# Narrow experts' postponed split and a final layer norm without GpSimd in a backbone layer with 32 experts

## The chip, the cores and the metric

The kernel runs on one core of a Trainium2 chip. The metric is the device time of one execution in microseconds. Engines are named TensorE (PE; its weight loads are PEld), VectorE (DVE), ScalarE (ACT), GpSimd (POOL) and SyncE (SP, which here only starts DMAs).

## The reference

One layer on 1024 latent tokens of width 1024: a state space branch and a window attention branch, a residual and a layer norm, then a mixture of 32 experts (4 per token), a second residual and the last layer norm. What the change touches is this end:

```python
gu = xb @ w_gate_up[e] + b_gate_up[e]
glu, lin = jnp.split(gu, 2, axis=-1)
act = glu * jax.nn.sigmoid(SWIGLU_ALPHA * glu) * (lin + 1)   # after limits
return act @ w_down[e] + b_down[e]
...
h_new = layer_norm(DEEPNORM_ALPHA * h_new + g2 * ffn, ln2_g[l], ln2_b[l])
```

## The kernel before

The experts are sorted by how many tokens they have. Experts with room for more than 128 rows (ranks 0 to 14) are **wide**, the others have room for 128 and are **narrow**. `ORDER` takes them as 0, 31, 1, 30, ...: wide and narrow in turn, and at the end three narrow ones in a row. Each expert has 12 steps, `c` = 0 to 11, one for each chunk of 1 MB of its weights: eight gate/up chunks, then four down chunks.

Everything is computed in fp32 by parts. A chunk comes in two halves of 512 KB (`raw<-w_gate_up`, `raw<-w_down`, L1515, SyncE, into eight buffers). `Weights.prepare` splits each half: ScalarE copies it to the hi part `wh` (L1532), VectorE subtracts to get the lo part `wl` (L1534); that frees the raw buffer, and the next load may start. There are four buffers of split chunks: three chunks are prepared ahead, so step `c` prepares chunk `c + 3`, counted on into the next expert. TensorE multiplies hi by hi, lo by hi and hi by lo (L1347, L1348, L1350; wide up chunks L1400, L1401).

The orders of TensorE, VectorE and ScalarE are the program's (`manual_schedule`); SyncE's and GpSimd's are put by a scheduler. In each step `weave` takes one piece of each job in turn: the expert's own work `cur.after(c)`, `W.prepare()`, the next expert's x parts (`put`, L1325 and L1327, at c = 1, 6, 7, 10) and, in early experts, list building. Then `cur.main(c)` issues the matmuls:

```python
cur.before(c)
weave(prev.store(1) if c == 0 and prev else None, cur.after(c), W.prepare(), x, limit(to_lists, 1))
...
cur.main(c, W.ready.pop(0))
```

In a narrow expert each half of the activation is finished at c = 4 and c = 8 (`act`, L1385 and L1386 on VectorE, which read the result of the up chunks before). At c = 5 and c = 9 `before` has TensorE transpose it (`tp<-ident,t`, L1318), and `after` splits the transposed half (ScalarE L1325, VectorE L1327, `a<-tp,a`). Down chunks 8 and 9 use the first half, 10 and 11 the second.

An expert's rows are added to the result in HBM by GpSimd's indirect DMA (`acc_d<-y,tab`, L1483) at c = 0 of the next expert. The index tables of later experts (`tab<-list_d`, L1672) are loaded on SyncE's queue into five buffers, each free when the scatter that used it is over.

`finish` is the last layer norm, in four groups of two tiles of 128 rows: SyncE loads the tiles, VectorE makes the statistics (L78, L79) and the inverse root by small operations (`rsqrt`, L61 to L72), ScalarE normalizes (L1842), VectorE multiplies by the gain (L1843), GpSimd adds the bias (L1844), SyncE stores (L1845).

## Time and profile before

| | |
|---|---|
| median of 3 runs | 2726.91 us (2722.59 to 2729.72) |
| the profiled execution | 2724.81 us, span 2723.0 us |
| TensorE busy in the span | 2470.5 us (91%) |
| VectorE busy | 2136.4 us (78%) |
| ScalarE busy | 1480.4 us (54%) |
| GpSimd busy | 312.5 us (11%) |
| expert loop, first wide up matmul to last down matmul | 1100.64 to about 2655 us |
| final layer norm, first load to the end | 2670.97 to 2723.0 us |

Times in rows are microseconds from the start of the span. Busy shares are a mean over stages of different kinds; what a wait costs is read in its stage. A row of waits names the engine and line that waited, the one that ended the wait, and then total us, times, longest us. A row of a timeline gives start, duration, engine, line, operation, out<-in, count, and in brackets the idle time before it with what ended it. In a timeline "SPq" rows are DMAs being put on the queue.

### The profile page before, as it was taken

Reading aid. Unit: us, or ns where it says so; the run is one execution under the profiler, and the core shown is the slowest. Engines: PE = TensorE matmul, PEld = TensorE weight load, DVE = VectorE, ACT = ScalarE, POOL = GpSimd, SP = SyncE. Lnnn points to the kernel's source line nnn. Section 1 sums busy time; section 2 is a strip of 40 time slices with the busy share of each in tenths; the row PEclk is TensorE's granted clock in tenths of the full one; section 3 lists DMA queues with packets and bytes.
Section 4 is the critical chain, followed back from the end, with each engine's and each line's share of the span. In section 5 each row is a group of like instructions: output and inputs, shape, how many; then the busy total and the mean of one; then the engine's idle time right before and its main releaser. Section 6 shows DMA issues by size and latency. Waiting matters only on the chain. (4 is left out here: it accounts for less than half of the span.)

```text
span 2723.0 us, 40435 instructions
## 1 busy us (share of the span) xinstructions
PE 2470.5 (91%) x13750; PEld 2105.6 (77%) x13750; DVE 2136.4 (78%) x3818; ACT 1480.4 (54%) x2375; POOL 312.5 (11%) x205
## 2 busy tenths in 40 slices
PE   6799899888989987799999999999999999999990
PEld 2598887777778876678888888879878887888880
DVE  9635798237778868787988887988888898888995
ACT  0622112657757512555656666766666676667661
POOL 3300000000000004012220100111011011101003
PEclk8799999988999877899999999999999999999995
DMA  7534623544587672787978988988988999999984
GB/s 247 175 119 150 211 88 112 176 151 157 211 303 263 234 272 88 241 263 233 289 242 271 311 250 280 322 270 268 318 282 260 322 304 290 282 335 309 313 291 147
DMA packets 409699, 657.00 MB, mean 241 GB/s; under 512 B 42144, under 2 KB 213024, under 8 KB 403904
## 3 DMA queue, kind: packets, MB, share of 16 engines
q1 hardware_dynamic: 396160, 610.25, 67.3%
q0 software_dynamic: 12896, 42.54, 6.8%
q8 instruction: 110, 1.80, 0.3%
q10 hardware_dynamic: 432, 1.57, 0.2%
q14 instruction: 101, 0.83, 0.1%
HBM read 565.05 MB, written 89.88 MB: 241 GB/s over the span
## 5 line engine op out<-in xcount | busy, mean ns | idle before, releaser
L1534 DVE TENSOR_TENSOR wl<-raw,wh 128x1024 fp32r<-128x1024 f32 x768 | 923.6, 1219 | 202.3 <-ACT wh L1532 189.4
L1532 ACT ACTIVATE wh<-raw 128x1024 fp32r<-128x1024 f32 x768 | 795.3, 1053 | 296.9 <-PE dn L1350 77.8
L1400 PE MATMUL uw<-x,wh 128*128 128x320 f32 (+5 forms) x1920 | 576.7, 364 | 0.2 <-issue 0.2
L1401 PE MATMUL uw<-x,wl 128*128 128x192 f32 (+4 forms) x1920 | 500.3, 261 | 0.0
L1400 PEld LDWEIGHTS uw<-x,wh 128*128 128x128 f32 x1920 | 362.9, 189 | 24.0 <-issue 0.3
L1401 PEld LDWEIGHTS uw<-x,wl 128*128 128x128 f32 x1920 | 368.1, 192 | 0.6
L1347 PE MATMUL dn<-wh,a 128*128 128x512 f32 (+4 forms) x752 | 297.9, 396 | 0.0
L1348 PE MATMUL dn<-wl,a 128*128 128x512 f32 (+4 forms) x752 | 294.6, 392 | 0.0
L1350 PE MATMUL dn<-wh,a 128*128 128x512 f32 (+3 forms) x608 | 239.7, 394 | 0.6 <-DVE a L1327 0.6
L1347 PE MATMUL up<-wh,x 128*128 128x512 f32 x544 | 217.8, 400 | 0.0
L1350 PE MATMUL up<-wh,x 128*128 128x512 f32 x544 | 213.0, 391 | 0.0
L1348 PE MATMUL up<-wl,x 128*128 128x512 f32 x544 | 212.0, 390 | 0.0
L1412 ACT ACTIVATE t<-uw,bias 128x160 f32<-128x160 f32 (+5 forms) x240 | 97.9, 420 | 136.8 <-PE uw L1401 136.6
L1347 PEld LDWEIGHTS dn<-wh,a 128*128 128x128 f32 (+4 forms) x752 | 136.6, 182 | 34.6
L1348 PEld LDWEIGHTS dn<-wl,a 128*128 128x128 f32 (+4 forms) x752 | 136.5, 182 | 34.5
L1483 POOL DMA_INDIRECT acc_d<-y,tab x35 | 80.5, 2299 | 566.9 <-DVE y L1481 463.6
L1350 PEld LDWEIGHTS dn<-wh,a 128*128 128x128 f32 (+3 forms) x608 | 113.5, 187 | 28.8 <-DVE a L1327 3.1
L1350 PEld LDWEIGHTS up<-wh,x 128*128 128x128 f32 x544 | 102.1, 188 | 22.1
L1347 PEld LDWEIGHTS up<-wh,x 128*128 128x128 f32 x544 | 102.5, 188 | 20.2
L1348 PEld LDWEIGHTS up<-wl,x 128*128 128x128 f32 x544 | 102.3, 188 | 19.6
L51 PE MATMUL mm<-whi,uh 128*128 128x256 f32 x320 | 108.3, 338 | 4.5 <-DVE r L308 4.5
L52 PE MATMUL mm<-wlo,uh 128*128 128x256 f32 x320 | 107.5, 336 | 0.0
(544 smaller groups left out, 4934.2 us busy)
## 6 DMA issues: line engine op xcount, KB each, us to landing
raw<-w_gate_up SPq DMA_DIRECT2D x512, 512.0 KB
raw<-w_down SPq DMA_DIRECT2D x256, 512.0 KB
mw<-w_mod SPq DMA_DIRECT2D x64, 256.0 KB
raw<-w_in SPq DMA_DIRECT2D x13, 1024.0 KB
raw<-w_mod SPq DMA_DIRECT2D x8, 1024.0 KB
gate_d<-gs SPq DMA_DIRECT2D x16, 512.0 KB
raw<-w_o SPq DMA_DIRECT2D x8, 1024.0 KB
x<-xhat_d SPq DMA_DIRECT2D x28, 256.0 KB
```

Of the source, the lines that this page charges most:

```text
L51: nc.tensor.matmul(out, lhsT=lsel(lh, k), rhs=rsel(rh, k), start=start and k == 0, stop=False)
L52: nc.tensor.matmul(out, lhsT=lsel(lh, k), rhs=rsel(rl, k), start=False, stop=False)
L1347: nc.tensor.matmul(ps, lhsT=h, rhs=wh[:, k], start=st, stop=False)
L1348: nc.tensor.matmul(ps, lhsT=h, rhs=wl[:, k], start=False, stop=en and nb <= 64)
L1350: nc.tensor.matmul(ps, lhsT=X[:, k0 + k, lo:lo + nb], rhs=wh[:, k], start=False, stop=en)
L1400: nc.tensor.matmul(p[:, 0:2 * n], lhsT=wh[:, k, fs], rhs=self.x[:, k, 0:2 * n], start=k == 0, stop=False)
L1401: nc.tensor.matmul(p[:, 0:m], lhsT=wl[:, k, fs], rhs=self.x[:, k, 0:m], start=False, stop=k == KT - 1)
L1412: nc.scalar.activation(out=y[i], in_=self.uw[i][:, 1], func=ACTF.Identity, bias=self.bias[:, q * 8 + j0 + i:q * 8 + j0 + i + 1])
L1483: nc.gpsimd.indirect_dma_start(out=K.acc_d, out_offset=bass.IndirectOffsetOnAxis(ap=wi[0:nb], axis=0), in_=o[0:nb], in_offset=None, bounds ...
L1532: nc.scalar.activation(out=h, in_=r, func=ACTF.Copy)
L1534: nc.vector.tensor_tensor(l, r, h, ALU.subtract)
```

## The change

In the expert loop, a narrow expert no longer prepares a chunk at c = 7; the next wide expert prepares two at c = 2, and `owed` keeps the count (the narrow expert at place 29 of the order is the last that postpones). At c = 8 and c = 9 of a narrow expert its own work is issued to the end before the weights are split. In `finish` all tiles are loaded first, three of them from ScalarE's queue; VectorE makes the statistics of the even tiles, ScalarE those of the odd ones by sums; the four even and the four odd inverse roots are each made at once; and VectorE does the rest in two scalar_tensor_tensor per tile, the last tile in two halves.

```diff
--- before.py
+++ after.py
@@ -1705,6 +1705,7 @@
                 weave(W.prepare())
                 cur.constants()
             prev = None
+            owed = False
             to_lists = spread(tc, K, P.li)
             with tc.manual_schedule(engines={mybir.EngineType.PE, mybir.EngineType.DVE, mybir.EngineType.Activation}):
                 for i in range(len(ORDER)):
@@ -1714,7 +1715,16 @@
                             ls = next(lists(i + 2, oh) or iter(()), None)
                         x = next(xs, None) if c in (1, 6, 7, 10) else None
                         cur.before(c)
-                        weave(prev.store(1) if c == 0 and prev else None, cur.after(c), W.prepare(), x, limit(to_lists, 1))
+                        late = not cur.wide and c == 7 and not owed
+                        owed = owed or late
+                        if not cur.wide and c in (8, 9):
+                            weave(cur.after(c))
+                            weave(W.prepare(), x, limit(to_lists, 1))
+                        else:
+                            weave(prev.store(1) if c == 0 and prev else None, cur.after(c), None if late else W.prepare(), x, limit(to_lists, 1))
+                        if cur.wide and c == 2 and owed:
+                            owed = False
+                            weave(W.prepare())
                         if c == 2:
                             oh = place(i + 2)
                         if c == 8:
@@ -1815,34 +1825,46 @@
 
 
 def finish(tc, a, o, K):
+
     nc = tc.nc
     v = nc.vector
     with ExitStack() as es:
         cp = es.enter_context(tc.tile_pool(name="fc", bufs=1))
         hp = es.enter_context(tc.tile_pool(name="fh", bufs=8))
         sm = es.enter_context(tc.tile_pool(name="fs", bufs=2))
+        hs = []
+        for t in range(8):
+            h = hp.tile([128, D], F32, tag="h", name="h")
+            (nc.scalar if t in (1, 3, 5) else nc.sync).dma_start(out=h, in_=K.acc_d[t * 128:(t + 1) * 128, :])
+            hs.append(h)
         gb = cp.tile([128, 2, D], F32, name="gb")
-        nc.scalar.dma_start(out=gb, in_=a["ln2"].unsqueeze(0).to_broadcast([128, 2, D]))
-        for g in range(4):
-            mv = sm.tile([128, 2, 2], F32, tag="mv", name="mv")
-            r = sm.tile([128, 2], F32, tag="r", name="r")
-            b = sm.tile([128, 2], F32, tag="b", name="b")
-            hs = []
-            for i in range(2):
-                t = g * 2 + i
-                h = hp.tile([128, D], F32, tag="h", name="h")
-                nc.sync.dma_start(out=h, in_=K.acc_d[t * 128:(t + 1) * 128, :])
-                ln_stats(nc, sm, h, mv[:, i], "l2")
-                hs.append(h)
-            rsqrt(nc, sm, r, mv[:, :, 1], 2, "l2")
-            v.scalar_tensor_tensor(b, mv[:, :, 0], -1.0, r, ALU.mult, ALU.mult)
-            for i in range(2):
-                t = g * 2 + i
-                h = hs[i]
-                nc.scalar.activation(out=h, in_=h, func=ACTF.Identity, scale=r[:, i:i + 1], bias=b[:, i:i + 1])
-                v.tensor_tensor(h, h, gb[:, 0], ALU.mult)
-                nc.gpsimd.tensor_tensor(h, h, gb[:, 1], ALU.add)
-                nc.sync.dma_start(out=o["out"][t * 128:(t + 1) * 128, :], in_=h)
+        nc.sync.dma_start(out=gb, in_=a["ln2"].unsqueeze(0).to_broadcast([128, 2, D]))
+        mv = cp.tile([128, 4, 2], F32, name="mv")
+        var = cp.tile([128, 4], F32, name="var")
+        neg = cp.tile([128, 2, 4], F32, name="neg")
+        sums = cp.tile([128, 2, 4], F32, name="sums")
+        junk = cp.tile([128, D], F32, name="junk")
+        for i in range(4):
+            ln_stats(nc, sm, hs[2 * i], mv[:, i], "l2")
+            h = hs[2 * i + 1]
+            nc.scalar.activation(out=junk, in_=h, func=ACTF.Identity, accum_out=sums[:, 0, i:i + 1])
+            nc.scalar.activation(out=neg[:, 1, i:i + 1], in_=sums[:, 0, i:i + 1], func=ACTF.Copy, scale=-1.0 / D)
+            nc.scalar.activation(out=junk, in_=h, func=ACTF.Square, bias=neg[:, 1, i:i + 1], accum_out=sums[:, 1, i:i + 1])
+        nc.scalar.activation(out=var, in_=sums[:, 1], func=ACTF.Copy, scale=1.0 / D)
+        for odd in range(2):
+            r = cp.tile([128, 4], F32, name="r%d" % odd)
+            if not odd:
+                v.tensor_scalar(neg[:, 0], mv[:, :, 0], -1.0, None, ALU.mult)
+            rsqrt(nc, sm, r, var if odd else mv[:, :, 1], 4, "l2")
+            for i in range(4):
+                t = 2 * i + odd
+                h = hs[t]
+                for c in ((0, 1) if t == 7 else (slice(0, 2),)):
+                    cols = slice(c * 512, c * 512 + 512) if t == 7 else slice(0, D)
+                    x = h[:, cols]
+                    v.scalar_tensor_tensor(x, x, neg[:, odd, i:i + 1], gb[:, 0, cols], ALU.add, ALU.mult)
+                    v.scalar_tensor_tensor(x, x, r[:, i:i + 1], gb[:, 1, cols], ALU.mult, ALU.add)
+                    nc.sync.dma_start(out=o["out"][t * 128:(t + 1) * 128, cols], in_=x)
 
 
 def mod_cols(tc, a, K, xp, tmp):
```

The first place is VectorE's order in a narrow expert (place 15 of the order, the one of the example below), from c = 6 to the next wide expert. `wl` are weight differences, `t` the activation, `a<-tp,a` and `x<-tp,x` differences of transposed halves. Before:

```order
L1382 TENSOR_TENSOR t<-up,t 128x512
L1534 TENSOR_TENSOR wl<-raw,wh 128x1024
L1327 TENSOR_TENSOR x<-tp,x 128x4x128
L1534 TENSOR_TENSOR wl<-raw,wh 128x1024 x2
L1327 TENSOR_TENSOR x<-tp,x 128x4x64
L1385 TENSOR_SCALAR t<-up 128x512
L1386 SCALAR_TENSOR_TENSOR t<-t 128x512
L1534 TENSOR_TENSOR wl<-raw,wh 128x1024 x3
L1327 TENSOR_TENSOR a<-tp,a 128x4x128
L1534 TENSOR_TENSOR wl<-raw,wh 128x1024 x3
L1327 TENSOR_TENSOR x<-tp,x 128x4x64
```

and with the change:

```order
L1382 TENSOR_TENSOR t<-up,t 128x512
L1534 TENSOR_TENSOR wl<-raw,wh 128x1024
L1327 TENSOR_TENSOR x<-tp,x 128x4x128
L1327 TENSOR_TENSOR x<-tp,x 128x4x64
L1385 TENSOR_SCALAR t<-up 128x512
L1386 SCALAR_TENSOR_TENSOR t<-t 128x512
L1534 TENSOR_TENSOR wl<-raw,wh 128x1024 x2
L1327 TENSOR_TENSOR a<-tp,a 128x4x128
L1534 TENSOR_TENSOR wl<-raw,wh 128x1024 x4
L1327 TENSOR_TENSOR x<-tp,x 128x4x64
```

The two weight differences between the last two x parts have left, and the activation difference stands ahead of one weight difference more.

The second place is SyncE's queue in the wide expert that follows: weight halves and the table loads (ISA rows belong to the addresses of the loads). Before:

```order
L1515 DMA raw<-w_gate_up 128x4x256
L1515 ISA
L1515 DMA raw<-w_gate_up 128x4x256
L1515 ISA
L1515 DMA raw<-w_gate_up 128x4x256
L1672 DMA tab<-list_d 128x4
L1672 DMA tab<-list_d 32x4
L1515 ISA
L1515 DMA raw<-w_down 128x2x512
L1515 ISA
L1515 DMA raw<-w_down 128x2x512
```

and with the change:

```order
L1515 DMA raw<-w_gate_up 128x4x256
L1515 ISA
L1515 DMA raw<-w_gate_up 128x4x256
L1515 ISA
L1515 DMA raw<-w_gate_up 128x4x256
L1672 DMA tab<-list_d 128x4
L1515 ISA
L1515 DMA raw<-w_gate_up 128x4x256
L1515 ISA
L1515 DMA raw<-w_gate_up 128x4x256
L1515 ISA
L1515 DMA raw<-w_down 128x2x512
```

The table load now stands ahead of the last two gate/up halves (in nine wide experts it does), and the load of the second table was put out earlier in that expert.

The third place is VectorE's end of the final layer norm. Before, from the last products but three:

```order
L1843 TENSOR_TENSOR h<-h,gb 128x1024
L1838 SCALAR_TENSOR_TENSOR b<-mv,r 128x2
L1843 TENSOR_TENSOR h<-h,gb 128x1024
L70 TENSOR_TENSOR l2t<-l2y 128x2
L71 TENSOR_TENSOR l2t<-l2t,l2v 128x2
L1843 TENSOR_TENSOR h<-h,gb 128x1024 x2
L72 SCALAR_TENSOR_TENSOR l2y<-l2t,l2y 128x2
L70 TENSOR_TENSOR l2t<-l2y 128x2
L71 TENSOR_TENSOR l2t<-l2t,l2v 128x2
L72 SCALAR_TENSOR_TENSOR r<-l2t,l2y 128x2
L1838 SCALAR_TENSOR_TENSOR b<-mv,r 128x2
L1843 TENSOR_TENSOR h<-h,gb 128x1024 x2
```

and with the change, where the odd tiles begin:

```order
L1866 SCALAR_TENSOR_TENSOR h<-h,r_26787,gb 128x1024 x2
L61 TENSOR_SCALAR l2v<-var 128x4
L1865 SCALAR_TENSOR_TENSOR h<-h,neg,gb 128x1024
L63 TENSOR_SCALAR l2y<-l2v 128x4
L1865 SCALAR_TENSOR_TENSOR h<-h,neg,gb 128x1024
L64 TENSOR_SCALAR l2y<-l2y 128x4
L65 TENSOR_SCALAR l2v<-l2v 128x4
L1865 SCALAR_TENSOR_TENSOR h<-h,neg,gb 128x1024
L70 TENSOR_TENSOR l2t<-l2y 128x4
L1865 SCALAR_TENSOR_TENSOR h<-h,neg,gb 128x512
L71 TENSOR_TENSOR l2t<-l2t,l2v 128x4
L1865 SCALAR_TENSOR_TENSOR h<-h,neg,gb 128x512
```

The products have become scalar_tensor_tensor, and the second inverse root is made in between the first ones of the odd tiles.

## Rows read from the trace of the kernel before

**Rows 1.** TensorE's waits, expert loop: who waited, total us, times, longest us.

```profile
PE tp L1318 <- DVE t L1386: 30.0, 14, 3.6
```

**Rows 2.** TensorE timeline, transposes at c = 5 of the first and third narrow expert.

```profile
1198.31 0.66 PE L1318 MATMUL tp<-ident,t 128*128 128x128 f32 x4 [1.47 <-DVE t L1386]
...
1415.10 0.66 PE L1318 MATMUL tp<-ident,t 128*128 128x128 f32 x4 [0.93 <-DVE t L1386]
```

**Rows 3.** Windows of two narrow experts; last columns PEclk, DMA share, GB/s.

```profile
1892.46:1935.08 42.62, 39.12 (x174) 31.34 (x172) 36.78 (x42) 28.60 (x33) 7.52 (x4) 0.96 0.93 291
1703.36:1740.53 37.17, 37.17 (x173) 30.27 (x172) 35.04 (x39) 28.07 (x32) 7.43 (x4) 1.00 0.98 310
```

**Rows 4.** TensorE timeline, the 42.62 us narrow expert and the next wide one.

```profile
1917.64 0.39 PE L1347 MATMUL dn<-wh,a 128*128 128x512 f32 x1
...
1924.02 0.63 PE L1318 MATMUL tp<-ident,t 128*128 128x128 f32 x4 [3.49 <-DVE t L1386]
...
1972.36 0.41 PE L1347 MATMUL dn<-wh,a 128*128 128x512 f32 x1
```

**Rows 5.** VectorE timeline, the same narrow expert.

```profile
1917.45 1.22 DVE L1534 TENSOR_TENSOR wl<-raw,wh 128x1024 fp32r<-128x1024 f32 x1
1918.58 0.68 DVE L1327 TENSOR_TENSOR x<-tp,x 128x512 fp32r<-128x512 f32 x1
1919.23 1.23 DVE L1534 TENSOR_TENSOR wl<-raw,wh 128x1024 fp32r<-128x1024 f32 x1
1920.99 1.23 DVE L1534 TENSOR_TENSOR wl<-raw,wh 128x1024 fp32r<-128x1024 f32 x1 [0.53 <-ACT wh L1532]
1922.13 0.42 DVE L1327 TENSOR_TENSOR x<-tp,x 128x256 fp32r<-128x256 f32 x1
1922.46 0.68 DVE L1385 TENSOR_SCALAR t<-up 128x512 f32<-128x512 f32 x1
1923.18 0.69 DVE L1386 SCALAR_TENSOR_TENSOR t<-t 128x512 f32<-128x512 f32 x1
```

**Rows 6.** ScalarE timeline, the same: weight copies and the loads they waited for.

```profile
1918.14 1.06 ACT L1532 ACTIVATE wh<-raw 128x1024 fp32r<-128x1024 f32 x1 [1.04 <-DMA raw<-w_down]
...
1919.89 1.06 ACT L1532 ACTIVATE wh<-raw 128x1024 fp32r<-128x1024 f32 x1 [0.42 <-DMA raw<-w_down]
...
1922.63 1.06 ACT L1532 ACTIVATE wh<-raw 128x1024 fp32r<-128x1024 f32 x1 [0.24 <-DMA raw<-w_down]
```

**Rows 7.** SyncE timeline, DMA issues of the same expert and the next.

```profile
1885.72 11.82 SPq L1515 DMA_DIRECT2D raw<-w_gate_up  x6
1904.56 0.34 SPq L1672 DMA_DIRECT2D tab<-list_d  x1
...
1948.26 0.82 SPq L1672 DMA_DIRECT2D tab<-list_d  x2
```

**Rows 8.** Groups of instructions, 2665 to 2724 us: count, busy us, mean ns, idle.

```profile
L1844 POOL TENSOR_TENSOR h<-h,gb 128x1024 f32<-128x1024 f32 x8 | 22.3, 2802 | 39.3 <-DVE h L1843 35.6 <-DVE b L1838 3.8
...
L1842 ACT ACTIVATE h<-h,b,r 128x1024 f32<-128x1024 f32 x8 | 9.5, 1232 | 56.7 <-DVE b L1838 56.7
```

**Rows 9.** Timeline of all engines, the final layer norm.

```profile
2670.97 4.36 SPq L1834 DMA_DIRECT2D h<-acc_d  x8
2676.33 1.29 DVE L78 BATCH_NORM_STATS2 l2st<-h 128x6 f32<-128x512 f32 x2 [20.27 <-DMA h<-acc_d]
...
2687.58 2.34 DVE L1843 TENSOR_TENSOR h<-h,gb 128x1024 f32<-128x1024 f32 x2
...
2689.84 2.30 DVE L70 TENSOR_TENSOR l2t<-l2y 128x2 f32<-128x2 f32 x1
...
2711.04 0.16 DVE L1838 SCALAR_TENSOR_TENSOR b<-mv,r 128x2 f32<-128x2 f32 x1
...
2713.81 5.55 POOL L1844 TENSOR_TENSOR h<-h,gb 128x1024 f32<-128x1024 f32 x2 [3.21 <-DVE h L1843]
```

**Rows 10.** Line L1386: count, duration ns min/median/max, first and last start, forms.

```profile
L1386 DVE SCALAR_TENSOR_TENSOR t<-t x34: 691/692/707, 1197.6 to 2645.4; 128x512 f32<-128x512 f32 x34
```

## The prediction, made before the changed kernel was run

> **What bounds the kernel now.** I read the waits of TensorE first, then single narrow experts in the windows and in the timelines of TensorE, VectorE, ScalarE and SyncE, then the last 52 us.
>
> In the expert loop TensorE has almost one wait left. It stops 14 times, 30.0 us in all, in front of the transposes of a narrow expert's activation, and each time the releaser is L1386, the last VectorE operation of that activation [rows 1]. Three of the 14 are at step c = 5 of the first three narrow experts, 1.47, 1.47 and 0.93 us (the first and the last of them are in [rows 2]); the change does not touch that step. The other 11 are at c = 9, together 30.0 - 3.9 = 26.1 us.
>
> A stop at c = 9 makes a narrow expert longer: 42.62 us against 37.17 for one without it [rows 3]. The longer one also shows a granted clock of 0.96, so part of it ran at 1.2 instead of 2.4 GHz, right after the stop: 4% of 42.6 is 1.7 us. One other narrow expert has that clock; so 26.1 + 2 x 1.7 = 29.5 us is what the stops at c = 9 cost.
>
> Why VectorE is late there is seen in the 42.62 us expert. TensorE begins chunk 8 at 1917.64, so the activation could start then; the transposes behind it start at 1924.02 after a wait of 3.49, so it was over by 1920.5 [rows 4]. Meanwhile VectorE, which takes its instructions in order, makes the lo parts of chunk 10, two instructions at 1919.23 and 1920.99 with a hole before the second, and starts the activation at 1922.46 [rows 5]. Chunk 10's data were late: ScalarE waited for the DMA of its first half until 1918.14 [rows 6]. SyncE had put out no weight load between 1897.54 (1885.72 + 11.82) and 1904.56, because a small table load stood in front of them [rows 7]. DMA is not the bound of the whole loop, though: over such an expert it moves 291 GB/s, against 310 in the undisturbed one [rows 3].
>
> After the loop TensorE rests, and VectorE and GpSimd form one chain: loads from 2670.97, statistics from 2676.33, last GpSimd addition over at 2713.81 + 5.55 = 2719.37, end at 2723.0 [rows 9]. Two costs stand out. GpSimd needs 2.8 us for an addition [rows 8] of the same size as a VectorE product of 1.2, and a VectorE operation on 128x2 numbers takes 2.30 us while GpSimd works on an addition [rows 9].
>
> **Narrow experts: what moves.** Nothing is removed; per narrow expert two splits (two ScalarE copies of 1.05, two VectorE differences of 1.15 to 1.2 us) leave step 7 and come back in step 2 of the next wide expert, and at c = 9 one activation difference passes one weight difference. With them the two weight loads that they release move too. I replay the 42.62 us expert with its own durations:
> - VectorE ends chunk 9 at 1918.58, then the two x differences (0.61 + 0.34) at 1919.5, then the activation (0.72 + 0.69) at 1920.95 [rows 5]. The transposes were possible at 1920.5 and start at about 1921.0: a stop of 0.5 us in place of 3.49, and I take the low clock behind it as gone too.
> - Chunk 10's lo parts come next, 1920.95 to 1923.2 (data there since 1919.9 [rows 6]), then the activation difference, 1923.8. TensorE wants both at 1921.0 + 0.4 (transposes) + 2.75 (chunk 9) = 1924.2: in time by 0.4 us.
> - Chunk 11 was landed by 1922.63 [rows 6], its lo parts end at 1926.1; TensorE wants them at 1927.4. Chunk 12 ends at 1928.5 and is wanted at 1930.2. So with two chunks of lead instead of three TensorE still runs through, by 0.4 to 1.7 us.
>
> This is the worst of the 11. In the four others with late data I take up to 0.3 each by the same sum, and where the stop was 1.2 to 2.2 the 2.3 us taken out of step 7 cover it. I take 1.3 us in all as left: 29.5 - 1.3 = **28.2 us** gained. Bounds: 18 if half of the five late-data stops come back elsewhere; 33.4 if the three at c = 5 go too.
>
> In the wide expert the two splits add 2.3 us to VectorE at step 2. A wide step is (1972.36 - 1935.08) / 8 = 4.66 us of TensorE [rows 4], its results are buffered for two chunks, and the lag is worked off over the later steps and the down part; I cost it at nothing, and if that cover failed it would be at most 2.3 us in each of 15 wide experts. The last three experts are narrow in a row; the first of them postpones a chunk that no wide expert makes up, so the lead stays at two to the end. The postponed work only shifts, and I cost it at nothing.
>
> **The final layer norm, step by step.** Gone are 8 GpSimd additions, 8 ScalarE normalizations and 8 VectorE products. VectorE now has:
> - statistics of 4 tiles, from 2676.33 as before: 4 x 1.43 (1.29 for two halves [rows 9], the rest for the aggregate) = 5.7;
> - 14 dependent operations on four columns at 0.2 us each (such a one lasts 0.16 [rows 9], and I add 0.04 to the next): 2.8;
> - 16 scalar_tensor_tensor of 128x1024, two of them halved: two products of that size in a row take 2.34 [rows 9], so 1.16 each: 18.6;
> - the second chain of 13 small ones, of which five stand between large ones: 2.1.
>
> Sum 29.2, so VectorE ends at 2705.5. ScalarE's part (4 x two passes of 1.23 [rows 8] and a few short ones, about 12 us) ends near 2688, before the odd tiles need it. The last store was 3.6 us from its releaser to the end; with half the bytes I take 3.0. End 2708.5, **14.5 us** earlier. Bounds 11 to 17: gb is now the last load and may come 1 us after it is wanted, h0 may land 1 us earlier or later, and small operations cost 0.07 to 0.2.
>
> On the large term there is a rule that speaks against the change. The row: L1386, a scalar_tensor_tensor on two fp32 inputs in SBUF, takes 692 ns for 512 columns [rows 10], which is the pace of the product (1.2 for 1024 [rows 9]). The Trainium skill (Vector Engine (DVE) Microarchitecture Reference, Points that are easy to get wrong) says that scalar_tensor_tensor with two non-bf16 SBUF sources runs at half throughput. By that rule the 16 would take about 36 instead of 18.6 us; the row does not show it.
>
> **Sum.** 28.2 + 14.5 = 42.7 us. The profiled execution took 2724.81, so 2682.1; the median of the runs shown is 2.1 above it: 2684.
>
> **Rivals.**
> - *The lead of two is too short.* For: in the replay chunk 10 and the activation difference are ready 0.4 us before they are wanted, and DMA was late in that place. Against: the data of chunks 10 and 11 had landed. The five late-data experts lose 5 x 3.4 us in stops (3.0 to 3.6 each; 3.6 is the longest [rows 1]) and 3.4 in clock; if half of that comes back, 10 us are missing: 2694.
> - *The loop gains nothing*, because VectorE then waits somewhere before the activation for the same late data. Against: nothing between chunk 9 and the activation reads weights any more. Only the 14.5 would be left: 2712.
> - *scalar_tensor_tensor at half pace* on two inputs of 1024 columns: 18.6 us more in the last stage, and the time 2703. Against it: 512 columns show the full pace [rows 10].
> - *Slower: the table load.* In 9 wide experts the table load now stands ahead of the last two gate/up halves on SyncE's queue. Before, it was released 1948.26 - 1935.08 = 13.2 us after the wide expert began [rows 4, 7]. The chunk behind it (number 7) is wanted 7 x 4.66 = 32.6 us after that begin; up to 8 halves at 350 GB/s need 12 us to land, so there are about 8 us to spare. To eat up 42.7 us, each of the nine must stop for 4.8, which needs a release 12.8 us later than now; then the time would be 2727, and each further us costs 9: with 2 us more, 2745. What speaks for it is only that the scatter in front of the table load shares its time with more VectorE work.
>
> **How the numbers follow.** Forecast 0.76, short lead 0.11, loop gains nothing 0.05, half pace 0.05, table load 0.03. My own case reaches from 2724.81 - (33.4 + 17) + 2.1 = 2676 to 2727 - (18 + 11) = 2698, which takes in the short lead; with 2 us on both sides for the scatter of the runs (2722.6 to 2729.7) the range is 2674 to 2700. A measurement of this kernel can tell 0.3%, 8 us. All cases but the table load come out faster by more; the loop-gains-nothing case is nearest to no change. Faster 0.94, same 0.03, slower 0.03.
>
> **What would show it.** Right: the c = 9 waits on L1386 fall from 26.1 to some 1 or 2 us while the three at c = 5 stay (3.9 us); all narrow experts last about 37 us at a clock of 1.00; wide experts keep their length; from the first load to the end 37 to 38 us instead of 52, with VectorE busy throughout and scalar_tensor_tensor rows of about 1.2 us. Wrong: a wait of TensorE on lo parts at c = 10 or 11 or at the start of a wide expert; wide experts grown by the catch-up; a SyncE wait on the table load much over 8 us; or scalar_tensor_tensor rows of 2.2 us.

## The result, and the profile after

The changed kernel took **2676.82 us** (median of 4 runs, 2673.99 to 2678.92), against 2724.75 for the kernel before in the same session (4 runs, 2719.12 to 2729.72): a ratio of 0.9824, 95% interval 0.9803 to 0.9844. The forecast was 2684, with a range from 2674 to 2700. So the sign, the size and the range held. Whether the reasons held is another question, and the runs below answer it differently for the two halves of the forecast.

The two profiled executions, stage by stage (the span of the changed one is 2672.2 us):

| stage | before | after | difference | forecast |
|---|---|---|---|---|
| ahead of the expert loop (code not touched) | 1100.6 | 1094.7 | -5.9 | 0 |
| expert loop, first wide up matmul to last down matmul | 1554.4 | 1523.1 | -31.3 | -28.2 |
| loop end to SyncE's first load of the final layer norm | 16.0 | 13.8 | -2.1 | 0 |
| SyncE's first load of the final layer norm to the end | 52.0 | 40.6 | -11.4 | -14.5 |

The first line is no gain: where the loop begins lay anywhere between 1088.6 and 1102.2 us in the executions profiled for this study, all with the same code up to there. The loop and the end are what the change did. The loop's length has a scatter of its own: in other executions with the same loop code, of kernels shown below, the old loop took 1555.0 and 1563.7 us and the new one 1519.9 and 1527.6. Its gain is therefore somewhere between 27 and 44 us, and the 31.3 of this pair is one value of it.

TensorE's waits in the loop of the changed kernel (who waited for whom, total us, times, longest us), to be held against [rows 1]:

```profile
PE tp L1318 <- DVE t L1386: 5.5, 5, 1.8
```

The five are the three at c = 5 (1.47, 1.47, 1.84) and two remainders at c = 9 of 0.32 and 0.42. The worst expert of before [rows 3] in the same view (PE, PEld, DVE, ACT, POOL busy, then clock, DMA share, GB/s):

```profile
1876.51:1913.91 37.40, 37.39 (x173) 30.19 (x172) 34.42 (x40) 26.72 (x31) 8.37 (x4) 1.00 0.91 282
```

It went from 42.62 to 37.40 us, TensorE is busy in all of it, and the clock is 1.00 where it was 0.96 behind the stop. DMA still moves only 282 GB/s: the data are no earlier. Why that costs nothing now is seen on VectorE and ScalarE, in a timeline of the same expert (the counterparts of [rows 5, 6]):

```profile
1899.42 1.05 ACT L1532 ACTIVATE wh<-raw 128x1024 fp32r<-128x1024 f32 x1
1900.81 1.22 DVE L1534 TENSOR_TENSOR wl<-raw,wh 128x1024 fp32r<-128x1024 f32 x1
1901.94 1.02 DVE L1327 TENSOR_TENSOR x<-tp,x 128x512 fp32r<-128x512 f32 x2
1902.87 0.68 DVE L1385 TENSOR_SCALAR t<-up 128x512 f32<-128x512 f32 x1
1903.59 0.69 DVE L1386 SCALAR_TENSOR_TENSOR t<-t 128x512 f32<-128x512 f32 x1
1903.61 1.06 ACT L1532 ACTIVATE wh<-raw 128x1024 fp32r<-128x1024 f32 x1 [1.68 <-DMA raw<-w_down]
1904.20 2.36 DVE L1534 TENSOR_TENSOR wl<-raw,wh 128x1024 fp32r<-128x1024 f32 x2
```

The next weight copy still waits 1.68 us for its load, until 1903.61. But the weight difference that depends on it now stands behind the activation in VectorE's queue, so the activation goes ahead at 1902.87. That is the step the forecast described.

The final layer norm of the changed kernel, all engines (to be held against [rows 9]; ACTq are DMAs put on ScalarE's queue):

```profile
2630.67 1.32 ACTq L1838 DMA_DIRECT2D h<-acc_d  x3
2631.63 2.36 SPq L1838 DMA_DIRECT2D h<-acc_d  x5
2634.19 1.06 ACT L1850 ACTIVATE junk<-h 128x1024 f32<-128x1024 f32 x1 [22.05 <-DMA h<-acc_d]
...
2638.96 1.29 DVE L78 BATCH_NORM_STATS2 l2st<-h 128x6 f32<-128x512 f32 x2 [17.64 <-DMA h<-acc_d]
...
2646.95 0.16 DVE L72 SCALAR_TENSOR_TENSOR r<-l2t,l2y 128x4 f32<-128x4 f32 x1
2647.03 2.47 DVE L1865 SCALAR_TENSOR_TENSOR h<-h,neg,gb 128x1024 f32<-128x1024 f32 x2
...
2663.31 5.00 DVE L1866 SCALAR_TENSOR_TENSOR h<-h,r,gb 128x1024 f32<-128x1024 f32 x5
```

VectorE never stops from 2638.96 to 2668.31, and the end comes 3.9 us later. But it starts 7.3 us after SyncE issued its first tile, where it was 5.4 before. ScalarE's three tiles were issued 1.0 us ahead of SyncE's, and its first was there 3.5 us after its issue.

### The profile page after: what moved, and what is told of

It reads as the page before. It is cut to its first block, busy times and chain, and to the rows that moved or that the text cites. A ratio compares the mean times of both kernels' runs of the same rounds, so it can differ in the third digit from the quotient of the medians.

```text
span 2672.2 us, 40422 instructions
## 1 busy us (share of the span) xinstructions
PE 2450.6 (92%) x13750; PEld 2093.3 (78%) x13750; DVE 2123.0 (79%) x3787; ACT 1477.4 (55%) x2388; POOL 294.3 (11%) x197
```

## The experiments

Twelve kernels were run. My theory of the loop was that of the forecast: weight differences in front of the activation, some of them with late data. Its rivals: the order at c = 8 and 9 does the work, the late data are all there is to it, or the smaller lead alone. Beside each time stands that of the kernel before from the same session, which differs by some us from one session to the next; what one run shows is therefore read from its stages.

### The two halves alone

The expert loop of the change with the old `finish`; and the old loop with the new `finish`.

> The loop as in the change, the final layer norm as in the kernel before. Theory (the gain is the lo work taken out of the way of the activation): the c = 9 waits of TensorE on L1386 fall from 26 us to about 1, the expert loop lasts 31 us less (1523 instead of 1554), the time is 28 to 32 us below the kernel before, ratio near 0.989. Rival (part of what the change gained in the loop hangs on the shorter end, or is spread of the stages ahead of the loop): the loop gains 25 or less and the stages ahead of it keep the 5.9 us that they were shorter.

> The loop as in the kernel before, the final layer norm as in the change. Theory: the loop lasts 1554 us with its 11 stops at c = 9, and from the first load to the end it takes 40 to 41 us instead of 52; the time is 11 to 14 us lower, ratio near 0.995. Rival (the two parts help each other): the sum of the gains of this run and of the loop alone misses the gain of both by more than 4 us.

Loop alone: 2690.5 us, ratio 0.987 (0.9838 to 0.9901). Its loop took 1527.6 us, 26.8 less than in the kernel before, so between the theory's 31 and the rival's 25. Its waits on L1386 are:

```profile
PE tp L1318 <- DVE t L1386: 6.7, 5, 2.8
```

A sixth wait of 1.46 us, at c = 5 of the first narrow expert, is put down to L1385 by the view. At c = 9 2.4 us are left.

Final layer norm alone: 2711.16 us, ratio 0.9941 (0.9912 to 0.997). Its waits on L1386 stayed at 29.6 us in 14, yet its loop took 1563.7 us and not the 1554 expected: five narrow experts show a granted clock of 0.92 to 0.96 here, against two in the kernel before. From SyncE's first load to the end it took 40.6 us, the same as in the changed kernel. The two halves add: 1.3% and 0.6% beside 1.8% together. In this kernel SyncE's loads were issued together with ScalarE's, and the first statistics began 4.2 us later instead of 7.3:

```profile
2671.10 2.92 SPq L1828 DMA_DIRECT2D h<-acc_d  x5
2671.24 1.58 ACTq L1828 DMA_DIRECT2D h<-acc_d  x3
2675.34 1.29 DVE L78 BATCH_NORM_STATS2 l2st<-h 128x6 f32<-128x512 f32 x2 [18.29 <-DMA h<-acc_d]
2678.67 1.29 DVE L78 BATCH_NORM_STATS2 l2st<-h 128x6 f32<-128x512 f32 x2 [1.80 <-DMA h<-acc_d]
```

It then waited for its second and third tile instead (1.80 and 1.03 us), so nothing was won in the end: the order in which tiles are issued decides who gets the first ones, not how long all of them take.

### The order at c = 8 and 9 alone, and the change without it

```diff
+                        if not cur.wide and c in (8, 9):
+                            weave(cur.after(c))
+                            weave(W.prepare(), x, limit(to_lists, 1))
```

> The kernel before with the changed order of c = 8 and c = 9 alone; nothing is postponed. Theory: the waits at c = 9 come from what stands ahead of the activation, and the order behind it does nothing: 24 to 28 us of waits stay and the loop lasts 1550 to 1558 us. Rival (the activation difference one weight difference earlier is part of the gain): the loop is shorter by 3 us or more.

> The change with the old order of c = 8 and c = 9: one chunk is postponed, the activation difference at c = 9 stands behind one weight difference as before. Theory: with one more weight difference (1.2 us) ahead of it the activation difference is ready 0.8 us too late in the experts with late data, so 2 to 6 us of the gain are lost in waits at c = 10; elsewhere nothing. Rival (the order is free): narrow experts keep their 37 to 38 us, the loop lasts 1523 to 1524.

With these lines alone in the kernel before: 2721.76 us (one run), 31.0 us of waits in 14, so they take none of the stops away; its loop of 1560.2 us, longer than the 1550 to 1558 expected, lies within the scatter of the old loop. The last three narrow experts are 1.1 us shorter. The change without them: 2683.34 us (one run), loop 1528.1 us, waits on L1386 of 6.9 us in 5. The waits of 2 to 6 us at c = 10 that I expected did not come; there are three of 0.3 us. What the three lines are worth shows in the last three narrow experts, which no wide one separates: 36.38, 36.41 and 35.50 us without them, 35.70, 35.82 and 34.93 with them, together 1.8 us. The rest of the loop's gain comes from the postponing.

### Why the data are late: the index tables' loads

```diff
-                    x = P.li.tile([128, 4], I32, tag="tab%d" % b, bufs=5, name="tab")
+                    x = P.li.tile([128, 4], I32, tag="tab%d" % b, bufs=24, name="tab")
```

This is the kernel before with that line only, so no table load has to wait for a scatter:

> The kernel before, with one edit: 24 buffers for the index tables instead of 5, so that their loads need not wait for a scatter in SyncE's queue. It asks why the data of chunk 10 are late at c = 8 in five narrow experts. Theory A (a table load in SyncE's queue holds the weight loads behind it): SyncE's waits for the scatter (92 to 103 us in the kernel before and in the changed one) nearly vanish, the five longest waits of TensorE on L1386 (3.0 to 3.6 us) shrink to 1.3 to 2.2 as in the other experts, the low clock behind them goes, and waits on L1386 sum to 17 to 22 us instead of 30; the loop is 8 to 13 us shorter. Rival B (the loads are late because the transfers themselves are slow there, or because raw buffers come free late): SyncE's waits on the scatter go and the waits of TensorE stay at 28 to 31 us. Either way at least 17 us of waits stay, since VectorE still makes chunk 10's lo parts ahead of the activation.

It took 2700.38 us (one run; the kernel before beside it 2718.79). The waits fell much further than either theory said:

```profile
PE tp L1318 <- DVE t L1386: 11.6, 6, 3.0
```

All six are in the first three narrow experts (there the table loads now come in one lot, from 1390.6 to 1458.8 us, and the third of these experts took 45.3 us for 41.2). From the fourth narrow expert on there is none, not even in the four where the stop had been 1.2 to 2.2 us and where the forecast had VectorE's own work stop TensorE. A second edit keeps five buffers and moves the loads in place of hoisting them:

```diff
-                    nc.sync.dma_start(out=x[0:nb], in_=K.list_d[r * LIST + b * 128:r * LIST + b * 128 + nb])
+                    nc.gpsimd.dma_start(out=x[0:nb], in_=K.list_d[r * LIST + b * 128:r * LIST + b * 128 + nb])
```

> The kernel before, with one edit: the index tables are loaded from GpSimd's queue, where the scatters they wait for are issued anyway, and not from SyncE's; still five buffers. TensorE's, VectorE's and ScalarE's orders are those of the kernel before, instruction for instruction, so any change of the loop comes from SyncE's queue alone. Theory A (all waits at c = 9 after the third narrow expert are late data behind a held table load, as with 24 table buffers): waits on L1386 fall from 28 to 31 us to 9.5 to 12, all in the first three narrow experts; no narrow expert from the fourth on is over 37.6 us; the loop is 1528 to 1534 us against 1554, and the time 19 to 26 us under the kernel before. Rival B (with 24 buffers it was the new place of the loads, all put out early, and some waits return when they are spread over the loop again, or the x gathers and scatters behind them on GpSimd's queue are late): waits of 15 us or more, or TensorE waiting for x.

2693.65 us, ratio 0.9907 (0.9888 to 0.9925). Waits on L1386, and the place of the worst expert of before:

```profile
PE tp L1318 <- DVE t L1386: 8.0, 6, 1.6
...
1874.94:1912.33 37.39, 37.39 (x173) 30.28 (x172) 36.44 (x42) 28.17 (x33) 9.70 (x6) 1.00 1.01 315
```

TensorE, VectorE and ScalarE run the instructions of the kernel before in its order, and still that expert is down to 37.39 us, with DMA at 315 GB/s instead of 291. The eight down halves are put out from 1881.44 in one stretch, with no table load among them:

```profile
1879.64 0.37 SPq L1515 DMA_DIRECT2D raw<-w_gate_up  x1
1881.44 10.84 SPq L1515 DMA_DIRECT2D raw<-w_down  x8
1893.19 17.20 SPq L1515 DMA_DIRECT2D raw<-w_gate_up  x11
```

So the table load that held SyncE's queue [rows 7] was the cause of every stop at c = 9 from the fourth narrow expert on (eight stops, 19.8 us), not of five late ones only. The trace of the kernel before fits: each of these eight experts has a table load on SyncE's queue 11.9 to 12.9 us after its begin, and the narrow experts after the third that have no stop have none there. In the first three, 4.1 us stay at c = 9. The third's stop fell from 3.04 to 0.85 us, but it was 0.85 in an execution with the tables on SyncE's queue too, so that part may be scatter. One line in the old kernel gets a loop of 1528.6 us, 25.7 of the 31.3 us that the whole change gets in the profiled pair.

### How little lead is enough, and postponing without making up

Two chunks postponed (none prepared at c = 6 and 7, made up at c = 2 and 4 of the wide expert):

```diff
-                        late = not cur.wide and c == 7 and not owed
-                        owed = owed or late
+                        late = not cur.wide and c in (6, 7) and owed < 2
+                        owed += late
...
-                        if cur.wide and c == 2 and owed:
-                            owed = False
+                        if cur.wide and c in (2, 4) and owed:
+                            owed -= 1
```

> The changed kernel with two chunks postponed instead of one: a narrow expert prepares none at c = 6 and c = 7, and the next wide expert makes one up at c = 2 and one at c = 4, so the lead is one chunk at c = 8 to 11. It asks how near the lead of two is to its limit. Theory A (my replay: with a lead of two the lo parts are ready 0.4 to 1.7 us before TensorE wants them; a step has 3.1 us): with one chunk less of lead TensorE waits for lo parts or hi parts of the chunk at each step from c = 8 on and into the next wide expert, 1 to 3 us in each of 15 narrow experts, and the loop is 20 to 45 us longer than with one postponed. Rival B (the lead has slack that the replay does not see, as VectorE has idle time): no new waits, the loop within 4 us of that with one postponed (1523 to 1528 us).

2682.01 us (one run), loop 1524.3 us; the only waits on L1386 left are the three at c = 5 (3.9 us). Up to the last wide expert no matmul waits for lo parts: there rival B held. In the three narrow experts at the end, where no wide expert makes anything up, TensorE's weight loads (PEld) do wait for them (total us, times, longest us):

```profile
PEld up L1348 <- DVE wl L1534: 2.8, 7, 0.5
PEld dn L1348 <- DVE wl L1534: 1.7, 5, 0.5
```

These three experts took 109.1 us for 106.5 in the changed kernel. So a lead of one chunk is enough for a single narrow expert between two wide ones and too short for three in a row. A timeline of VectorE in a narrow expert between wide ones, at c = 8:

```profile
1907.32 0.69 DVE L1385 TENSOR_SCALAR t<-up 128x512 f32<-128x512 f32 x1 [1.69 <-PE up L1361]
1908.04 0.69 DVE L1386 SCALAR_TENSOR_TENSOR t<-t 128x512 f32<-128x512 f32 x1
1908.65 2.35 DVE L1534 TENSOR_TENSOR wl<-raw,wh 128x1024 fp32r<-128x1024 f32 x2
```

Here VectorE waits for TensorE, not the reverse: it stood ready 1.69 us before the up product was done. TensorE transposes at 1909.85 and begins chunk 9 after that. Its first half's lo parts are done at 1909.8, the second's at 1911.0, and TensorE takes the halves one after the other. My replay had asked for both halves at the start of a step.

Then the change with its catch-up taken out, so that the lead falls to two chunks once and every later narrow expert prepares at c = 7 again:

```diff
-                        if cur.wide and c == 2 and owed:
-                            owed = False
-                            weave(W.prepare())
```

> The changed kernel with the first narrow expert's postponed chunk never made up: the lead is two chunks from there to the end, and every later narrow expert prepares a chunk at c = 7 again. It tells apart what the postponing does: Theory A (what counts is that no weight difference is queued between the matmuls of chunk 7 and the activation at c = 8): with the chunk prepared at c = 7 back in place, its two lo parts stand ahead of the activation again and waits of TensorE on L1386 at c = 9 come back, 1 to 3.6 us in most narrow experts, 20 to 35 us in all. Rival B (what counts is how far ahead, so how late the data are that VectorE is waiting for: with a lead of two the chunk prepared at c = 7 is chunk 9, whose data have long landed): waits on L1386 at c = 9 stay at or under 1.5 us each and under 12 us in all, and the loop stays within 8 us of 1523 to 1528 us.

2716.38 us (one run): the loop took 1559.1 us, so all of its gain is gone. Theory A held in eight of the sixteen later narrow experts, with stops at c = 9 of 1.6 to 5.0 us; the others run without one. TensorE's waits:

```profile
PE tp L1318 <- DVE t L1386: 29.0, 11, 5.0
```

The longest of them, with SyncE's queue, ScalarE and VectorE ahead of it:

```profile
1609.36 0.34 SPq L1672 DMA_DIRECT2D tab<-list_d  x1
1609.95 0.37 SPq L1515 DMA_DIRECT2D raw<-w_gate_up  x1
1616.55 0.46 SPq L1672 DMA_DIRECT2D tab<-list_d  x1
...
1617.88 6.99 SPq L1515 DMA_DIRECT2D raw<-w_down  x8
...
1628.88 1.06 ACT L1532 ACTIVATE wh<-raw 128x1024 fp32r<-128x1024 f32 x1 [2.92 <-DMA raw<-w_down]
...
1629.97 2.52 DVE L1534 TENSOR_TENSOR wl<-raw,wh 128x1024 fp32r<-128x1024 f32 x2 [1.85 <-ACT wh L1532]
...
1632.81 0.68 DVE L1385 TENSOR_SCALAR t<-up 128x512 f32<-128x512 f32 x1
...
1634.36 1.09 PE L1318 MATMUL tp<-ident,t 128*128 128x128 f32 x4 [4.99 <-DVE t L1386]
```

Two table loads hold the queue one after the other, the data come at 1628.88, the two weight differences at 1629.97, and only then the activation. The narrow expert with the stop of 4.19 us also has two such loads (2108.91 and 2116.30), and one of those without a stop has one (2204.60). The data were no earlier for being those of a nearer chunk; as I read it (no run shows it), because with a smaller lead the raw buffers come free later too, and the loads with them. Where the data are late, what counts is that nothing that reads weights stands between the up product and the activation.

### GpSimd's part in the end

The kernel before, with the bias added by VectorE (`v.tensor_tensor` in place of `nc.gpsimd.tensor_tensor` in L1844):

> The kernel before, with one edit in the final layer norm: the bias is added by VectorE instead of GpSimd. It asks how much of the shorter final layer norm (40.6 us from the first load to the end instead of 52.0) is GpSimd's going alone. Theory A (GpSimd's 2.8 us additions and the slow small VectorE operations beside them are the chain): the operations on 128x2 numbers take 0.1 to 0.2 us everywhere instead of up to 2.3, and the stage lasts 42 to 45 us, so 7 to 10 of the 11.4 us are GpSimd's going. Rival B (the gain is the new order: loads first, roots four at a time, normalization folded into scalar_tensor_tensor): the stage stays at 48 to 52 us, since VectorE gets eight additions of 1.2 us more. The loop is unchanged, waits on L1386 28 to 31 us.

2718.65 us (one run, 2718.79 beside it; one run can't tell 7 us). The stage can: 45.0 us from the first load to the end (2671.85 to 2716.9) instead of 52.0 (the old stage took 52.0 to 53.5 us in five executions). The operations on 128x2 numbers (count, duration min/median/max in ns), in the kernel before and then with this edit:

```profile
L70 DVE TENSOR_TENSOR l2t<-l2y x12: 107/153/2301, 2680.9 to 2708.4; 128x2 f32<-128x2 f32 x12
```

```profile
L70 DVE TENSOR_TENSOR l2t<-l2y x12: 105/152/161, 2682.1 to 2706.4; 128x2 f32<-128x2 f32 x12
```

With no GpSimd addition beside them none of the twelve is over 161 ns. So 7.0 of the 11.4 us are GpSimd's going, though VectorE has eight additions of 1.2 us more; the other 4.4 are the rest of the rewrite. The Trainium skill (SBUF — State Buffer, SBUF: two separate sides) has a rule for this: a VectorE operation with two SBUF inputs and a GpSimd operation that reads SBUF need one shared pair of ports, the first to start locks it, and the other waits for the whole instruction. The trace agrees: 2301 ns beside a GpSimd addition, 161 at most without one.

### The loads of the last stage, and a version of both

The change with tables from GpSimd's queue, and the change with tiles 0, 2, 4 on ScalarE's queue:

> The changed kernel, with the index tables loaded from GpSimd's queue. It asks what is left for the postponing once SyncE's queue is not held. Theory A (the postponing only takes the cost out of late data, and otherwise the work in front of the activation costs only the first three narrow experts): the loop is 1521 to 1525 us, so 0 to 3 us under the changed kernel's 1523 to 1528 and 5 to 10 under the kernel before with this edit (the first three narrow experts 5 us, the tail 1.5); time 2672 to 2680. Rival B (the table loads still cost the changed kernel something that shows as no wait of TensorE): 5 us or more under the changed kernel's 2676.8. Slower than 2682 would mean that GpSimd's queue is now what is late.

> The changed kernel, with another spread of the last loads: tiles 0, 2, 4 (whose statistics VectorE makes first) on ScalarE's queue, which starts first, and 1, 6, the gain and bias, 3, 5, 7 on SyncE's. In the changed kernel SyncE's first tile landed 7.3 us after its issue, ScalarE's first 3.5 us after. Theory A (the queue that starts first is served first, and VectorE's statistics wait for it): VectorE starts about 4 us after ScalarE's issue, that is 4.5 us earlier than now, and as it is busy from there to the end, the end comes 3.5 to 4.5 us earlier (36 to 37 us from the first load to the end instead of 40.6), if the odd tiles' sums on ScalarE, which now start later and take 12 to 13 us, are over before VectorE wants them 17 us after its start. Rival B (ScalarE's sums or the gain and bias come too late, or all tiles land later): less than 2 us.

With the tables moved: 2673.23 us, ratio 0.9823 (0.9803 to 0.9843), the changed kernel's own; loop 1521.4 us, the waits on L1386 only the three at c = 5. Once the late data cost nothing, taking them away brings nothing that can be measured. With the tiles spread anew: 2674.51 us, ratio 0.9836 (0.9818 to 0.9855), not shown to differ from the change. From the first issue, ScalarE's, to the end it is 40.0 us against 41.6 in the changed kernel, so rival B (less than 2 us). VectorE started 3.6 us after that issue as expected, then ran out of tiles twice:

```profile
2627.06 1.31 ACTq L1844 DMA_DIRECT2D h<-acc_d  x3
2628.08 0.36 SPq L1842 DMA_DIRECT2D gb<-ln  x1
...
2636.24 1.29 DVE L78 BATCH_NORM_STATS2 l2st<-h 128x6 f32<-128x512 f32 x2 [2.63 <-DMA h<-acc_d]
...
2639.12 1.29 DVE L78 BATCH_NORM_STATS2 l2st<-h 128x6 f32<-128x512 f32 x2 [1.36 <-DMA h<-acc_d]
```

The scheduler had put the 1 MB of gain and bias ahead of SyncE's tiles. So the last kernel loads those before the last scatter (its trace has that load at 2608.4 us), writes VectorE's order of the end by hand, takes the tables from GpSimd's queue, and for the three waits at c = 5 puts the one-hot tables of a later expert, which stood ahead of that activation, two steps later and its lists one step later:

```diff
-                        if c == 5:
+                        if c == (5 if cur.wide else 6):
                             ls = next(lists(i + 2, oh) or iter(()), None)
...
-                        if c == 2:
+                        if c == (2 if cur.wide else 4):
                             oh = place(i + 2)
...
+        gb = pool(es, "fgb").tile([128, 2, D], F32, name="gb")
+        nc.sync.dma_start(out=gb, in_=a["ln2"].unsqueeze(0).to_broadcast([128, 2, D]))
         rest(tc, a, K)
```

> The changed kernel with what the runs before this one point to, each in a stage of its own. (1) Index tables from GpSimd's queue. (2) In a narrow expert the one-hot tables and lists of a later expert are put two steps and one step later (c = 4 and 6), since they stand in front of the activation that TensorE waits for at c = 5 in the first three. (3) Final layer norm: gain and bias loaded before the end of the last expert's scatter; tiles 0, 2, 4 on ScalarE's queue, 6, 1, 3, 5, 7 on SyncE's; VectorE's order written by hand, with the first root between the first products and the second root between the last ones of the first half. Theory A: the three waits at c = 5 (3.9 us) fall to 0 to 1 us and no wait on L1386 is left over 0.5, so the loop is 1516 to 1521 us against 1521.4 with (1) alone; VectorE starts 3.6 us after ScalarE's first load is issued, is never idle for over 1 us, needs 27.5 us, and the end is 35 to 36.5 us after that issue (41.5 in the changed kernel, 39.9 with the other spread alone). Together 7 to 11 us under the changed kernel's 2676.8: 2666 to 2670. Rival B: the transfers, not VectorE, set the pace of the final layer norm (4 MB of loads at the 313 GB/s they had take 13.4 us, so the odd tiles' sums on ScalarE end 24 us or more after the first issue, and VectorE waits for them), and it stays at 38 us or more; or the later lists make the gather of a later expert's rows late, which shows as TensorE waiting for x: then 2671 to 2677.

**2667.02 us** (6 runs, 2663.86 to 2670.75), ratio 0.9796 (0.9774 to 0.9818): 9.8 us under the changed kernel's median, which is from another session, and the fastest of all. The waits (lines are one lower here, L1385 is L1386 above) and the end:

```profile
PE tp L1317 <- DVE t L1385: 1.4, 4, 0.4
```

```profile
2624.88 1.37 ACTq L1869 DMA_DIRECT2D h<-acc_d  x3
2625.98 2.41 SPq L1869 DMA_DIRECT2D h<-acc_d  x5
2628.60 1.29 DVE L78 BATCH_NORM_STATS2 l2st<-h 128x6 f32<-128x512 f32 x2 [12.51 <-DMA h<-acc_d]
...
2653.26 5.00 DVE L1887 SCALAR_TENSOR_TENSOR h<-h,r,gb 128x1024 f32<-128x1024 f32 x5
```

Two of the four waits are at c = 5. The loop took 1519.95 us, but the changed kernel's own loop also took 1519.9 in the execution with the tiles spread anew, so a shorter loop as a whole is not shown. From ScalarE's first load to the end it is 37.2 us, over the 35 to 36.5 expected, against 41.6 in the changed kernel, all of it from VectorE's start (3.7 us after the issue against 8.3). VectorE itself took 29.7 us, as in the changed kernel (29.4) and not the 27.5 expected of the order by hand: its third tile came 0.67 us late, and what the interleaved roots saved is no more than that.

## Why the prediction was right, and where only its number was

**How far the sum is luck.** In the profiled pair the forecast 28.2 + 14.5 = 42.7 us meets a measured 31.3 + 11.4 = 42.7, because two misses of 3 us cancel. The pair differs by 50.8 us all the same (the medians by 47.9): of the rest, 5.9 us lie in code that was not touched and 2.1 between the loop and the loads of the final layer norm.

**The stops at c = 9: 26.1 plus 3.4 us of clock, less 1.3.** Measured: waits of 30.0 fell to 5.5 us, the clock of 0.96 is gone from both experts, and what was left at c = 9 is 0.74 us where I had 1.3. The three at c = 5 stayed, as said; the third was 1.84 for 0.93. The loop gained 31.3, inside 18 to 33.4. The 3.1 us over the forecast are the three experts in a row at the end, 1.4 us, which I had costed at nothing and where the new order at c = 8 and 9 works, and pieces of 0.6 us or less in other narrow experts. The clock term of two experts was that of one execution: with the same old loop and as many stops, five experts had the lower clock in another, and the loop took 9.3 us more. That the size came so near is in part luck of the execution that was profiled.

**The cause was half right.** That chunk 10's lo parts stood ahead of the activation, and that the data behind a held queue were late, are both in the runs. But I took late data for the cause of five stops, and the differences' own 2.3 us for that of the others. The step that failed is "where the stop was 1.2 to 2.2 the 2.3 us taken out of step 7 cover it": with the tables off SyncE's queue, VectorE does those 2.3 us in the same place and nothing stops. All stops from the fourth narrow expert on were late data. Only those at c = 9 of the first three, 4.1 us, are left to VectorE's own work: moving the tables leaves them, and the change takes them away. That it is VectorE's work there is concluded from this and not tested by itself.

**The replay's margins of 0.4 to 1.7 us were too small.** They led me to give a short lead a chance of 0.11. A lead of one chunk ran without a wait on lo parts wherever a wide expert follows, and cost 2.6 us in the three narrow experts in a row. The error was to want both halves of a chunk at the start of its step; that the margin does run out is right, only a chunk later.

**Wide experts at nothing.** Right: from the fifth on they are within 0.2 us of before; the first four differ by -1.0 to +0.7 us, with both signs.

**The final layer norm, 14.5 forecast, 11.4 measured.** Statistics 5.7 us (2638.96 to 2644.67), as forecast. First root 2.33 for 2.8. The 16 scalar_tensor_tensor at 1.20 each (2.47 for two) for 1.16. From the last of them to the end 3.9 for 3.0. The mis-sized term is the start: I let it be "from 2676.33 as before", 5.4 us after the first load, and put 1 us on it in the bounds; it was 7.3. By the wording of the step, h0 may land 1 us earlier or later, and ScalarE's tiles ahead of it made it 2. How large the miss is depends on where one counts from. From the loop's end VectorE began after 21.2 us where it had been 21.3, because the loads were put out sooner (no run shows why), and the end came 13.6 us earlier.

**The rule on scalar_tensor_tensor.** The Trainium skill's half throughput for two fp32 sources in SBUF (Vector Engine (DVE) Microarchitecture Reference, Points that are easy to get wrong) did not show: 128x1024 took 1277 ns as a median, and 2.47 us for two, close to the pace of a product, 2.34 for two [rows 9]. The measurement decides.

**The table load as the slower rival.** It did not come: SyncE's waits for the scatter were 92.0 us in 17, the longest 8.5, after 103.1 in 17 and 7.9 in the kernel before. Yet the table load it named was the key to the loop, at a place ahead of the activation instead of in the wide expert.

## What to carry to other kernels

When an engine that works in order is late, follow the one operation it was held at back through the DMA to the queue that issued it: a small load with a long wait, put in the queue of the large loads, can stop TensorE, and moving that one load was the cheapest repair here. The other repair is to keep whatever needs such data behind the work that others wait for; where that is done, the lead can be smaller than a replay with whole chunks says, as long as something makes it up again. At the end of a kernel, price the arrival of the first tile with all the loads that are issued ahead of it, on every queue.

## What the runs showed of the hardware that I had not expected

- A table load of 0.34 us of issue time cost up to 3.6 us of TensorE through the queue behind it in the kernel before, and two in a row cost 5.0 in the kernel that never makes its chunk up. Where the granted clock fell after the stop (0.96 over the expert), 1.7 us came on top; after other stops of the same length (3.5 and 3.6 us) it did not fall.
- Which queue issues first decided whose tiles came first: with ScalarE's loads 1.0 us ahead, VectorE had SyncE's first tile of 512 KB 7.3 us after its issue (6.0 to 7.6 in five executions with this order); with SyncE's 0.14 us ahead it took 4.2.
- VectorE products of 128x2 numbers (two inputs) go from 0.15 us to as much as 2.3 us while GpSimd adds, and are 0.16 at most without it.
- Stages with the same code began up to 13.6 us apart in different executions, more than some of the effects studied here: compare stage by stage.
